# S5 of a hybrid decoder trunk with rows in the order (group, step, channel): block-diagonal products as pairs of 64x64 quadrants

## The chip, the cores and the metric

The kernel runs on one core of a Trainium2 chip. The metric is device time in microseconds (us): the median of three runs was 2262.53 us, the lowest 2256.43 and the highest 2264.71. The engines are PE (matrix products), PEld (the loading of the stationary operand into PE), DVE (vector), ACT (scalar and activation), POOL (GpSimd) and SP, whose queue issues every DMA of this kernel.

## What is computed

Two layers, 512 tokens, width 1024, float32. Each layer is a half-step FFN, a mixing sub-layer and another half-step FFN, all between RMSNorms. The mixer runs three parts on columns of one projection: A is RWKV-7 (4 heads of 64), C is a gated DeltaNet (4 heads of 128), and B, which the change touches, is S5:

```python
ug = u.reshape(bsz, t_len, S5_GROUPS, S5_GROUP_DIM)          # 16 groups of 16 channels
bu_re = jnp.einsum('btgh,gnh->btgn', ug, bbar_re)            # 64 complex states a group
bu_im = jnp.einsum('btgh,gnh->btgn', ug, bbar_im)
...
_, _, x_re, x_im = lax.associative_scan(_complex_linear_combine, elems, axis=1)
y = (jnp.einsum('btgn,ghn->btgh', x_re, c_re) - jnp.einsum('btgn,ghn->btgh', x_im, c_im)
     + d_skip.reshape(S5_GROUPS, S5_GROUP_DIM) * ug)
z = jax.nn.gelu(y.reshape(bsz, t_len, S5_WIDTH))
return z * jax.nn.sigmoid(z @ w_glu + b_glu)
```

No product of S5 crosses from one group of 16 channels to another.

## The kernel before, in words

Each layer is worked in two halves of 256 tokens, so that one half's mixer can be filled up with the other half's FFN. The string `steps` in `run` names the stages: A and B are the FFNs, P the projection, M the mixers, O the output projection, with layer and half behind the letter (M01 is layer 0, half 1). A framework's scheduler, which runs a model of the chip while the kernel is built, sets the order of the instructions on every engine. The order is fixed once built: each engine and the DMA queue of SP take theirs strictly in turn, so an instruction that has to wait holds up all behind it on its engine. A changed piece moves rows elsewhere in the program as well.

The FFN is the bulk. `up` and `down` multiply in three parts (`mm3`, lines 245 to 247): a weight tile `raw` of 256 KB comes by DMA, ACT rounds it to `whi` (line 226) and DVE computes the rest `wlo` (line 227); `ph`, `pp` and `acc` are the sums in PSUM. There are six `raw` buffers and four each of `whi` and `wlo`.

S5 takes its 256 tokens as 64 segments (`NC5`) of 4 steps (`CH5`), and its 16 groups as 8 pairs. For a pair the 128 rows of the input tile `U4` are ordered (step s, group of the pair g, channel c), 4 x 2 x 16. The state product (line 1271) multiplies 128 input rows with 128 states (2 groups x 64) for the real and the imaginary part, `lv5`; the output product (lines 1313 to 1315) goes from the two parts of the states and from `U4` to 128 output rows, with `lx5`. Since groups do not mix, half of each of these 128x128 matrices is zero. All have 64 moving columns (the segments) and are plain float32, for which the trace records two weight loads and two matmuls for each matmul of the program.

Once a layer, inside the FFN stages A00 and A10, `s5_setup` works the matrices out and stores them in DRAM (`s5w`): POOL copies each power of the matrices into zeroed tiles `Bx` and `Q` (lines 1192 and 1220), PE turns `Bx` (line 1207) and multiplies `Q` with `rep` for the tap products `pk5` (line 1238), DVE adds them to `K5` (line 1245).

In each M stage, `s5` writes its input to DRAM in eight DMAs, reads it back as `U4` in one DMA (line 1259), reads three tables (line 1264), four tiles `lv5` (line 1268) and four tiles `lx5` (line 1310), and sends its result over DRAM in four DMAs (line 1325). In the trace the digits of these names are left out: `v` is `v5` or the state product, `y` is `y5`, `U` is `U4` or `U5`.

Two helpers that S5 shares the M stage with matter for prices. `inverse2` has products of 64x64 quadrants, all in one quadrant at a time (lines 632 and 639). In `rwkv` the function `pair` (line 763) issues products of two groups of 64 rows in turn, one for each group, each into a PSUM bank of its own:

```python
ps = [self.mx([P, 2, 2, P], name) for _ in range(2)]
for j in range(2):
    for o in (1, 0):
        q = slice(64 * o, 64 * o + 64)
        m = nc.tensor.matmul(ps[o][:, j], a[q, j, c], ar[q, j, c], start=True, stop=True)
```

`inverse` sends its blocks `ATg` over DRAM (line 568, then `blk`, line 571) on the same SP queue, right behind the tables of S5.

Of the kernel before, what the change touches and what calls it, by code (L numbers as in the profile page):

```python
# [12 lines left out]
F32 = mybir.dt.float32  # L13
# [3 lines left out]
AF = mybir.ActivationFunctionType  # L17
ALU = mybir.AluOpType
AX = mybir.AxisListType

P = 128
# [6 lines left out]
DEPTH = 2  # L28
# [7 lines left out]
NC5 = HALF // CH5  # L36

R_MU, R_W0, R_A0, R_KK, R_KA, R_RK, R_V0, R_BG = 0, 8, 10, 12, 14, 16, 18, 20
R_ARE, R_AIM, R_D, R_CONV, R_LDT, R_G0, R_G2, R_G4 = 22, 30, 38, 46, 96, 0, 8, 16


class Trunk:
# [52 lines left out]
    def constants(self):  # L95
        nc, c = self.nc, self.cst
# [17 lines left out]
        self.hind = self.band(2, 64, 64, 0, "hind")  # L114
        self.bd32 = self.band(4, 32, 32, 0, "bd32")
# [14 lines left out]
    def params(self, l):  # L130
        nc, io = self.nc, self.io
        L = self.Ls[l]
        rows = self.b1([P, P], "rows")
# [17 lines left out]
        for s in range(4):  # L151
            self.late(nc.sync.dma_start(out=rows[R_D:R_D + 8, 32 * s:32 * s + 32],
                                        in_=io["s5_d"][l].rearrange("(p q) -> p q", q=32)))
# [965 lines left out]
    def s5_setup(self, l):  # L1119
        nc, io, L = self.nc, self.io, self.Ls[l]  # L1120
# [57 lines left out]
        Pw = [(self.b1([P, 8, 16], "P0r"), self.b1([P, 8, 16], "P0i"))]  # L1178
        self.cmul(Pw[0][0], Pw[0][1], b16(cr), b16(ci), Bre, Bim, [P, 8, 16])
        Cc = []  # L1180
        for cl in L["C"]:
            pc = self.mx([P, P], "pc")
            nc.tensor.transpose(pc, cl.rearrange("p t n -> p (t n)"), self.ident)
            cc = self.b1([P, 8, 16], "cc")
            nc.vector.tensor_copy(cc.rearrange("p a b -> p (a b)"), pc)
            Cc.append(cc)
        W5 = self.s5w[l]

        Bx = [self.b4([P, 8, 4, 2, 16], "Bx") for _ in range(2)]
        for t in Bx:  # L1190
            self.late(nc.gpsimd.memset(t, 0.0))
        cp = lambda o, i: nc.gpsimd.tensor_scalar(o, i, 1.0, 0.0, ALU.mult, ALU.add)
        cur = Pw[0]
        for j in range(4):
            for z in range(2):
                for g in range(2):
                    q = slice(64 * g, 64 * g + 64)
                    cp(Bx[z][q, :, 3 - j, g], cur[z][q])
            if j < 3:
                nx = (self.b1([P, 8, 16], "Pr"), self.b1([P, 8, 16], "Pi"))  # L1200
                self.cmul(nx[0], nx[1], b16(abr), b16(abi), cur[0], cur[1], [P, 8, 16])
                cur = nx
        for z in range(2):
            for hp in range(2):
                pv = self.mx([P, 4, P], "plv")
                for p in range(4):
                    nc.tensor.transpose(pv[:, p], Bx[z][:, 4 * hp + p].rearrange("n s g c -> n (s g c)"), self.ident)
                lv = self.b2([P, 4, P], "lv")
                nc.scalar.activation(lv, pv, AF.Copy)
                nc.sync.dma_start(out=W5[:, 4 * hp:4 * hp + 4, z], in_=lv)  # L1210
        Q = [[self.b4([P, 4, 5, 32], "Q") for _ in range(2)] for _ in range(2)]
        for t in Q[0] + Q[1]:
            self.late(nc.gpsimd.memset(t, 0.0))
        cur = Cc
        for j in range(5):
            for z in range(2):
                for g in range(2):
                    q = slice(64 * g, 64 * g + 64)
                    for hp in range(2):
                        nc.gpsimd.tensor_scalar(Q[z][hp][q, :, j, 16 * g:16 * g + 16], cur[z][q, 4 * hp:4 * hp + 4],  # L1220
                                                1.0 - 2 * z, 0.0, ALU.mult, ALU.add)
            if j < 4:
                nx = (self.b1([P, 8, 16], "Qcr"), self.b1([P, 8, 16], "Qci"))
                self.cmul(nx[0], nx[1], b16(abr), b16(abi), cur[0], cur[1], [P, 8, 16])
                cur = nx
        for z in range(2):
            for hp in range(2):
                nc.sync.dma_start(out=W5[:, 4 * hp:4 * hp + 4, 2 + z], in_=Q[z][hp][:, :, 1:5].rearrange("n p j c -> n p (j c)"))

        for hp in range(2):  # L1230
            pk = self.mx([P, 4, P], "pk5")
            rep = [self.b2([P, 4, 4, 32], "rep") for _ in range(2)]
            for z in range(2):
                nc.scalar.activation(rep[z], Bx[z][:, 4 * hp:4 * hp + 4, 3].rearrange("n p g c -> n p (g c)").unsqueeze(2)
                                     .to_broadcast([P, 4, 4, 32]), AF.Copy)
            for p in range(4):
                for z in range(2):
                    nc.tensor.matmul(pk[:, p], rep[z][:, p].rearrange("n s c -> n (s c)"),
                                     Q[z][hp][:, p, 0:4].rearrange("n j c -> n (j c)"), start=z == 0, stop=z == 1)
            K = self.b2([P, 4, P], "K5")  # L1240
            nc.gpsimd.tensor_tensor(K, self.ident.unsqueeze(1).to_broadcast([P, 4, P]),
                                    pr[:, R_D + 4 * hp:R_D + 4 * hp + 4].unsqueeze(2).to_broadcast([P, 4, P]), ALU.mult)
            for s in range(4):
                q = slice(32 * s, 32 * s + 32)
                nc.vector.tensor_tensor(K[q, :, 32 * s:], K[q, :, 32 * s:], pk[q, :, 0:P - 32 * s], ALU.add)
            nc.sync.dma_start(out=W5[:, 4 * hp:4 * hp + 4, 4], in_=K)


    def s5(self, l, h, I, mixT):
# [3 lines left out]
        W5 = self.s5w[l]  # L1253
# [5 lines left out]
        nc.sync.dma_start(out=U4, in_=scr.rearrange("s q p c -> (s q) p c"))  # L1259
# [48 lines left out]
        for p2 in range(4):  # L1308
            lx = self.b4([P, 2, 3, P], "lx5")
            self.after(nc.sync.dma_start(out=lx, in_=W5[:, 2 * p2:2 * p2 + 2, 2:5]), scan)  # L1310
            for p in range(2):
                q = 2 * p2 + p
# [11 lines left out]
        for t in range(4):  # L1324
            nc.sync.dma_start(out=scz[t].rearrange("p q c -> q p c"), in_=s1[32 * t:32 * t + 32])
# [193 lines left out]
```

## Time and profile before

| what | value |
|---|---|
| runs, median (lowest to highest) | 2262.53 us (2256.43 to 2264.71) |
| profiled execution, its own time | 2262.76 us |
| its span, first to last instruction | 2261.0 us |
| mean granted TensorE clock | 0.992 |
| PE, PEld, DVE, ACT, POOL busy | 97%, 90%, 75%, 53%, 7% |
| HBM read and written | 387.09 MB and 13.63 MB |

A busy share is that of recorded instructions; matmuls overlap in the pipeline, so what a matmul takes from PE is the distance to the next one's start and not its own recorded length. The M stages lie at about 325 to 500, 665 to 880, 1440 to 1660 and 1785 to 2010 us, and the two set-ups at about 115 to 185 and 1040 to 1105 us.

### The profile page before, as it was taken

How to read it: one execution, taken by the hardware profiler on the slowest of the kernel's cores; microseconds unless marked ns; L12 is line 12 of the kernel's file. 1: busy time of each engine (PE TensorE's matmuls, PEld its weight loads, DVE VectorE, ACT ScalarE, POOL GpSimd, SP SyncE). 2: the span in 40 equal slices, each digit the busy share in tenths (PEclk: the TensorE clock that was granted, in tenths of full speed). 3: DMA queues.
4: the chain of work that ended last, by engine and by line, in shares of the span. 5: the costliest groups of instructions: out<-in, count | busy, mean ns of one | idle time of the engine just before them, and what ended most of it. 6: DMA issues, size and time to landing. Idle time of an engine off the chain costs nothing.

```text
span 2261.0 us, 44455 instructions
## 1 busy us (share of the span) xinstructions
PE 2204.1 (97%) x15800; PEld 2032.1 (90%) x15800; DVE 1688.2 (75%) x3779; ACT 1191.7 (53%) x2521; POOL 163.2 (7%) x372
## 2 busy tenths in 40 slices
PE   8999999999999999999999999999999899998998
PEld 7998999897979999799989999889979799997997
DVE  6697886867876967768776678878677878677665
ACT  5555764444744444555555557544456545455554
POOL 2032000001000001201300010000020000001000
PEclk9999999999999999999999999999999999999999
DMA  7776765654765744567656677556467556456665
GB/s 207 199 209 186 186 196 151 187 145 153 202 192 154 206 136 142 175 186 220 200 177 188 189 197 204 155 172 189 130 179 207 162 172 193 123 154 187 190 187 154
DMA packets 604963, 403.67 MB, mean 179 GB/s; under 512 B 63306, under 2 KB 534340, under 8 KB 604740
## 3 DMA queue, kind: packets, MB, share of 16 engines
q1 hardware_dynamic: 604740, 400.82, 61.3%
q8 instruction: 124, 2.03, 0.4%
q14 instruction: 99, 0.81, 0.1%
HBM read 387.09 MB, written 13.63 MB: 177 GB/s over the span
## 4 chain that ended last, share of the span: by engine, by line
PE 87%; DVE 5%; DMA 4%; issue 1%; ACT 1%; POOL 0%; SPq 0%; DVEq 0%; ACTq 0%; POOLq 0%
PE ph L247 14%; PE ph L246 14%; PE ph L245 14%; PE acc L245 7%; PE acc L246 7%; PE acc L247 7%; PE pp L245 4%; PE pp L247 4%; PE pp L246 4%; PE acc L1386 2%; DVE wlo L227 1%; PE xt L309 1%; DMA blk<-scr 1%; PE py L610 1%; DMA raw<-in_w_in 1%
## 5 line engine op out<-in xcount | busy, mean ns | idle before, releaser
L226 ACT ACTIVATE whi<-raw 128x512 fp32r<-128x512 f32 (+2 forms) x1296 | 813.2, 632 | 835.4 <-PE ph L246 401.3
L227 DVE TENSOR_TENSOR wlo<-raw,whi 128x512 fp32r<-128x512 f32 (+2 forms) x1296 | 889.1, 690 | 408.5 <-ACT whi L226 397.2
L245 PE MATMUL ph<-hth,whi 128*128 128x256 f32 x2464 | 701.5, 285 | 6.1 <-DVE gu L364 3.2
L247 PE MATMUL ph<-hth,wlo 128*128 128x256 f32 x2464 | 702.4, 285 | 4.4 <-DVE wlo L227 4.1
L246 PE MATMUL ph<-htl,whi 128*128 128x256 f32 x2464 | 701.3, 285 | 3.9 <-DVE htl L318 3.8
L245 PEld LDWEIGHTS ph<-hth,whi 128*128 128x128 f32 x2464 | 466.6, 189 | 18.5 <-issue 3.9
L246 PEld LDWEIGHTS ph<-htl,whi 128*128 128x128 f32 x2464 | 466.2, 189 | 14.1 <-DVE htl L318 5.5
L247 PEld LDWEIGHTS ph<-hth,wlo 128*128 128x128 f32 x2464 | 467.2, 190 | 11.7 <-DVE wlo L227 7.5
L246 PE MATMUL acc<-wlo,gh 128*128 128x512 f32 x704 | 275.6, 397 | 0.0
L247 PE MATMUL acc<-whi,gl 128*128 128x512 f32 x704 | 271.1, 398 | 0.0
L245 PE MATMUL acc<-whi,gh 128*128 128x512 f32 x704 | 257.4, 400 | 0.6 <-ACT whi L226 0.6
L247 PEld LDWEIGHTS acc<-whi,gl 128*128 128x128 f32 x704 | 131.6, 188 | 29.4 <-issue 0.7
L246 PEld LDWEIGHTS acc<-wlo,gh 128*128 128x128 f32 x704 | 132.0, 188 | 23.4 <-issue 0.7
L245 PEld LDWEIGHTS acc<-whi,gh 128*128 128x128 f32 x704 | 130.3, 189 | 22.5 <-ACT whi L226 0.8
L245 PE MATMUL pp<-hth,whi 128*128 128x256 f32 x352 | 99.6, 284 | 2.8 <-ACT whi L226 2.5
L245 PE MATMUL ph<-hx,whi 128*128 128x256 f32 x352 | 99.3, 282 | 0.9 <-DVE gu L364 0.9
L370 ACT ACTIVATE gh<-gu 128x256 fp32r<-128x256 f32 x176 | 71.7, 407 | 52.6 <-DVE gu L364 51.7
L246 PE MATMUL pp<-htl,whi 128*128 128x256 f32 x352 | 98.9, 282 | 0.4 <-DVE htl L318 0.4
L247 PE MATMUL pp<-hth,wlo 128*128 128x256 f32 x352 | 99.0, 283 | 0.3 <-DVE wlo L227 0.2
L247 PE MATMUL ph<-hx,wlo 128*128 128x256 f32 x352 | 99.2, 282 | 0.0
L246 PE MATMUL ph<-hx,whi 128*128 128x256 f32 x352 | 98.8, 281 | 0.0
L245 PE MATMUL pp<-hx,whi 128*128 128x256 f32 x352 | 98.7, 281 | 0.0
(492 smaller groups left out, 3355.0 us busy)
## 6 DMA issues: line engine op xcount, KB each, us to landing
raw<-in_ffn_w SPq DMA_DIRECT2D x1056, 256.0 KB
raw<-in_w_in SPq DMA_DIRECT2D x176, 256.0 KB
raw<-in_w_out SPq DMA_DIRECT2D x96, 256.0 KB
raw<-in_w_in SPq DMA_DIRECT2D x32, 260.0 KB
gain<-in_norm_gain SPq DMA_DIRECT2D x28, 256.0 KB
lx<-s5w SPq DMA_DIRECT2D x16, 384.0 KB
lv<-s5w SPq DMA_DIRECT2D x16, 256.0 KB
x<-in_x SPq DMA_DIRECT2D x4, 512.0 KB
```

The source lines that it names most:

```text
L226: nc.scalar.activation(hi, q, AF.Copy)
L227: nc.vector.tensor_tensor(lo, q, hi.bitcast(F32), ALU.subtract)
L245: mm(out, lh, rh, start=start, stop=False)
L246: mm(out, lh, rl, start=False, stop=False)
L247: mm(out, ll, rh, start=False, stop=stop)
L309: self.turned = nc.tensor.transpose(pt[:, kk, i * P:(i + 1) * P], xs[i][:, k * P:(k + 1) * P], self.ident)
L370: nc.scalar.activation(gh, u, AF.Copy, scale=0.5)
L610: nc.tensor.matmul(py[:, h], ATs[z][:, h], Xs[z][:, h].rearrange("p (q e k) -> p q e k", e=2, k=32)[:, :, 0, :], start=True, stop=True)
L1386: nc.tensor.matmul(accs[i][d], mixT[:, k, s], ws[d], start=k == 0, stop=k == KT - 1)
```

## The change

The rows of a pair of groups are now ordered (group, step, channel), so that the 64 rows of one group lie together. Every matrix of S5 is then two blocks of 64x64, and only these are built, stored, loaded and multiplied: a 128x128 product becomes two 64x64 products, one in the upper left and one in the lower right quadrant of the array, written in turn. Both write the same PSUM bank, the first partitions 0 to 63 and the second 64 to 127. `U4` is read in eight DMAs of 16 rows in place of one of 128, and the result is sent out in eight in place of four. `lv5` and `lx5` come in two DMAs each in place of four, with half the bytes. In the set-up the powers go from DVE straight into `Bx` and `Q`, so the zeroing and the copies on POOL are gone; the mask `e16` takes the place of partition slices where the taps are added.

```diff
+        Bx = [self.b2([P, 8, 4, 16], "Bx") for _ in range(2)]
+        at = lambda t, j: (t[0][:, :, j], t[1][:, :, j])
+        self.cmul(*at(Bx, 3), b16(cr), b16(ci), Bre, Bim, [P, 8, 16])
+        for j in (2, 1, 0):
+            self.cmul(*at(Bx, j), b16(abr), b16(abi), *at(Bx, j + 1), [P, 8, 16])
+        Q = [self.b4([P, 8, 5, 16], "Q") for _ in range(2)]
...
-        cp = lambda o, i: nc.gpsimd.tensor_scalar(o, i, 1.0, 0.0, ALU.mult, ALU.add)
...
-                    cp(Bx[z][q, :, 3 - j, g], cur[z][q])
...
-                        nc.gpsimd.tensor_scalar(Q[z][hp][q, :, j, 16 * g:16 * g + 16], cur[z][q, 4 * hp:4 * hp + 4],
-                                                1.0 - 2 * z, 0.0, ALU.mult, ALU.add)
...
+            self.cmul(*at(Q, j + 1), b16(abr), b16(abn), *at(Q, j), [P, 8, 16])
...
-                for z in range(2):
-                    nc.tensor.matmul(pk[:, p], rep[z][:, p].rearrange("n s c -> n (s c)"),
-                                     Q[z][hp][:, p, 0:4].rearrange("n j c -> n (j c)"), start=z == 0, stop=z == 1)
+        halves = (slice(0, 64), slice(64, P))
+        for p in range(8):
             for z in range(2):
+                for q in halves:
+                    nc.tensor.matmul(pk[q, p], rep[z][q, p].rearrange("n s c -> n (s c)"),
+                                     Q[z][q, p, 0:4].rearrange("n j c -> n (j c)"), start=z == 0, stop=z == 1)
...
-                nc.vector.tensor_tensor(K[q, :, 32 * s:], K[q, :, 32 * s:], pk[q, :, 0:P - 32 * s], ALU.add)
+            nc.vector.scalar_tensor_tensor(K[:, :, 16 * s:], pk[:, :, 0:64 - 16 * s], self.e16[:, s:s + 1], K[:, :, 16 * s:],
+                                           ALU.mult, ALU.add)
...
-        nc.sync.dma_start(out=U4, in_=scr.rearrange("s q p c -> (s q) p c"))
+        for g in range(2):
+            for s in range(4):
+                nc.sync.dma_start(out=U4[64 * g + 16 * s:64 * g + 16 * s + 16], in_=scr[s, 16 * g:16 * g + 16])
...
-        for p2 in range(4):
-            lv = self.mw.tile([P, 2, 2, P], F32, tag="lv5", name=self.n("lv5"), bufs=4)
-            self.after(nc.sync.dma_start(out=lv, in_=W5[:, 2 * p2:2 * p2 + 2, 0:2]), I["usi"])
-            for p in range(2):
+        for hp in range(2):
+            lv = self.mw.tile([P, 4, 2, 64], F32, tag="lv5", name=self.n("lv5"), bufs=4)
+            self.after(nc.sync.dma_start(out=lv, in_=WV[:, 4 * hp:4 * hp + 4]), I["usi"])
+            for p in range(4):
                 for z in range(2):
-                    nc.tensor.matmul(pv[z][:, 2 * p2 + p], lv[:, p, z], U4[:, 2 * p2 + p], start=True, stop=True)
+                    for q in halves:
+                        nc.tensor.matmul(pv[z][q, 4 * hp + p], lv[q, p, z], U4[q, 4 * hp + p], start=True, stop=True)
...
-                nc.tensor.matmul(py[:, q], lx[:, p, 2], U4[:, q], start=True, stop=False)
-                nc.tensor.matmul(py[:, q], lx[:, p, 0], X[0][:, q, 0:NC5], start=False, stop=False)
-                nc.tensor.matmul(py[:, q], lx[:, p, 1], X[1][:, q, 0:NC5], start=False, stop=True)
+                for k, m in ((2, U4[:, i]), (0, X[0][:, i, 0:NC5]), (1, X[1][:, i, 0:NC5])):
+                    for q in halves:
+                        nc.tensor.matmul(py[q, i], lx[q, p, k], m[q], start=k == 2, stop=k == 1)
...
-        for t in range(4):
-            nc.sync.dma_start(out=scz[t].rearrange("p q c -> q p c"), in_=s1[32 * t:32 * t + 32])
+        for g in range(2):
+            for t in range(4):
+                nc.sync.dma_start(out=scz[t, :, 16 * g:16 * g + 16].rearrange("p q c -> q p c"),
+                                  in_=s1[64 * g + 16 * t:64 * g + 16 * t + 16])
```

The order on PE around the state products of M00, before. A row is line, operation, output and inputs, and size of the output; `v` has two tiles, one for the real and one for the imaginary part.

```order
L246 MATMUL ph_6179<-htl_3072,whi_6188 128x256
L1271 MATMUL v_1085_4928<-U_1081_4920,lv_1087_4930 128x64 x2
L1271 MATMUL v_1085_4928<-U_1081_4920,lv_1088_4936 128x64 x2
L1271 MATMUL v_1085_4928<-U_1081_4920,lv_1089_4942 128x64 x2
L1271 MATMUL v_1085_4928<-U_1081_4920,lv_1090_4948 128x64 x2
L247 MATMUL ph_6179<-hth_3071,wlo_6189 128x256
```

The same place in the change: first the place where the first product of the state stands, then the one where the others begin.

```order
L250 MATMUL ph_6151<-hth_2957,whi_6190 128x256
L251 MATMUL ph_6151<-htl_2958,whi_6190 128x256
L1257 MATMUL v_1060_4864<-U_1056_4849,lv_1062_4866 64x64
L252 MATMUL ph_6151<-hth_2957,wlo_6191 128x256
L250 MATMUL ph_6151<-hth_2961,whi_6190 128x256
```

```order
L251 MATMUL ph_6151<-htl_2984,whi_6196 128x256
L1257 MATMUL v_1060_4864<-U_1056_4849,lv_1062_4866 64x64 x6
L1257 MATMUL v_1061_4865<-U_1056_4849,lv_1062_4866 64x64 x6
L1257 MATMUL v_1060_4864<-U_1056_4849,lv_1062_4866 64x64
L1257 MATMUL v_1061_4865<-U_1056_4849,lv_1062_4866 64x64 x2
L1257 MATMUL v_1060_4864<-U_1056_4849,lv_1063_4884 64x64 x2
```

One product of the upper quadrant now stands alone, 12 FFN matmuls ahead of the other 31, which follow one another with the two quadrants in turn. So it is in all four M stages (7 to 12 matmuls ahead). The output products stand as two pairs alone and then 22 pairs in one piece, where before two single ones were followed by pieces of 10 and 12, or of 10, 6 and 6.

The order on SP around the input of S5 in M00, before; a row's last part is the size of the destination.

```order
L221 DMA raw_6292<-in_ffn_w 128x4x128
L1259 DMA U_1081_4920<-s5u_4911 128x512
L1264 DMA T_1082_4922<-s5t_127 128x512
L1264 DMA U_1083_4923<-s5t_128 128x512
L1264 DMA M_1084_4924<-s5t_129 128x512
L221 DMA raw_6322<-in_ffn_w 128x4x128
L221 DMA raw_6328<-in_ffn_w 128x4x128
L221 DMA raw_6367<-in_ffn_w 128x512
L568 DMA scr_4834<-ATg_4786 32x8x32 x4
L571 DMA blk_4843<-scr_4834 64x1024
```

And in the change:

```order
L226 DMA raw_6264<-in_ffn_w 128x4x128
L1244 DMA U_1056_4849<-s5u_4840 16x512 x8
L1249 DMA T_1057_4858<-s5t_136 128x512
L1249 DMA U_1058_4859<-s5t_137 128x512
L1249 DMA M_1059_4860<-s5t_138 128x512
L573 DMA scr_4763<-ATg_4715 32x8x32 x4
L226 DMA raw_6294<-in_ffn_w 128x4x128
L226 DMA raw_6300<-in_ffn_w 128x4x128
L576 DMA blk_4772<-scr_4763 64x1024
```

One issue for `U4` has become eight, and no weight tile stands between the tables and `ATg`, where three did.

## Rows read from the trace of the kernel before

**Rows 1.** The page, part 1: busy time, share and instructions of each engine.
```profile
PE 2204.1 (97%) x15800; PEld 2032.1 (90%) x15800; DVE 1688.2 (75%) x3779; ACT 1191.7 (53%) x2521; POOL 163.2 (7%) x372
```

**Rows 2.** The page, part 4: shares of the chain that ended last.
```profile
PE 87%; DVE 5%; DMA 4%; issue 1%; ACT 1%; POOL 0%; SPq 0%; DVEq 0%; ACTq 0%; POOLq 0%
```

**Rows 3.** Groups by line: busy us, mean ns, then idle us before them and releaser.
```profile
L1271 PE MATMUL v<-U,lv 128*128 128x64 f32 x128 | 15.1, 271 | 0.0
...
L1313 PE MATMUL y<-U,lx 128*128 128x64 f32 x64 | 12.1, 270 | 1.6 <-DMA lx<-s5w 1.5
L1238 PE MATMUL pk<-Q,rep 128*128 128x128 f32 x64 | 11.3, 351 | 4.3 <-POOL Q L1220 4.3
```

**Rows 4.** PE in order of time, M00, state products: start us, length us, instruction.
```profile
390.21 0.28 PE L246 MATMUL ph<-htl,whi 128*128 128x256 f32 x1
390.33 1.89 PE L1271 MATMUL v<-U,lv 128*128 128x64 f32 x16
392.03 0.36 PE L247 MATMUL ph<-hth,wlo 128*128 128x256 f32 x1
```

**Rows 5.** PE in order of time, M00, output products: a piece of 20 records.
```profile
417.70 0.33 PE L1315 MATMUL y<-X5i,lx 128*128 128x64 f32 x2
...
419.85 0.48 PE L247 MATMUL acc<-whi,gl 128*128 128x512 f32 x1
```

**Rows 6.** PE in order of time, products of one 64x64 quadrant, M00 and M01.
```profile
491.44 0.28 PE L246 MATMUL ph<-htl,whi 128*128 128x256 f32 x1
491.64 1.14 PE L632 MATMUL py<-xb,AT 64*64 64x64 f32 x16
492.71 0.39 PE L247 MATMUL ph<-hth,wlo 128*128 128x256 f32 x1
...
825.48 2.08 PE L639 MATMUL pz<-W,Y 64*64 64x64 f32 x32
827.48 0.38 PE L247 MATMUL ph<-hth,wlo 128*128 128x256 f32 x1
```

**Rows 7.** PE in order of time: two row groups in turn, then one row group alone.
```profile
333.83 1.13 PE L763 MATMUL pk<-ar,ka 64*128 64x256 f32 x8
334.90 0.39 PE L245 MATMUL ph<-hth,whi 128*128 128x256 f32 x1
...
1430.98 1.12 PE L729 MATMUL pv<-vr,wv 32*128 32x256 f32 x4
1432.04 0.55 PE L715 MATMUL pn<-ident,rkk 128*128 128x128 f32 x3
```

**Rows 8.** PE in order of time, set-up of layer 0: transposes, then tap products.
```profile
160.95 1.09 PE L1207 MATMUL plv<-ident,Bx 128*128 128x128 f32 x8
161.79 0.37 PE L247 MATMUL ph<-hth,wlo 128*128 128x256 f32 x1
...
173.39 5.24 PE L1238 MATMUL pk<-Q,rep 128*128 128x128 f32 x30 [2.15 <-POOL Q L1220]
178.39 0.36 PE L247 MATMUL ph<-hth,wlo 128*128 128x256 f32 x1
```

**Rows 9.** DVE in order of time, set-up of layer 0: the last powers of `Q`.
```profile
169.52 0.28 DVE L1070 TENSOR_TENSOR Qci<-Qci,cm 128x128 f32<-128x128 f32 x1
```

**Rows 10.** SP's queue and PE in order of time, M00 and M10.
```profile
383.91 0.48 SPq L1259 DMA_DIRECT2D U<-s5u  x1
384.45 0.42 SPq L1264 DMA_DIRECT2D T<-s5t  x1
384.92 0.42 SPq L1264 DMA_DIRECT2D U<-s5t  x1
...
1496.00 0.49 SPq L1259 DMA_DIRECT2D U<-s5u  x1
...
1501.09 1.89 PE L1271 MATMUL v<-U,lv 128*128 128x64 f32 x16
```

**Rows 11.** The chain that ended last, in order of time: a piece of M00.
```profile
391.95 2.75 DMA scr<-ATg
```

More of the change, by code (lines that the diff above doesn't have):

```diff
@@ L151, in params @@
         for s in range(4):
-            self.late(nc.sync.dma_start(out=rows[R_D:R_D + 8, 32 * s:32 * s + 32],
-                                        in_=io["s5_d"][l].rearrange("(p q) -> p q", q=32)))
+            self.late(nc.sync.dma_start(out=rows[R_D:R_D + 8].rearrange("p (g s c) -> p g s c", g=2, s=4)[:, :, s],
+                                        in_=io["s5_d"][l].rearrange("(p g c) -> p g c", g=2, c=16)))
         put(R_CONV, io["gdn_conv_w"][l].rearrange("i (t c) -> (i t) c", c=P), 48)
@@ L1182, in s5_setup @@
+        Q = [self.b4([P, 8, 5, 16], "Q") for _ in range(2)]
+        for z, cl in enumerate(L["C"]):
             pc = self.mx([P, P], "pc")
             nc.tensor.transpose(pc, cl.rearrange("p t n -> p (t n)"), self.ident)
[L1184 to L1191, printed above, removed]
@@ new lines, in s5_setup @@
+        pk = self.mx([P, 8, 64], "pk5")
+        rep = [self.b2([P, 8, 4, 16], "rep") for _ in range(2)]
+        for z in range(2):
+            nc.scalar.activation(rep[z], Bx[z][:, :, 3].unsqueeze(2).to_broadcast([P, 8, 4, 16]), AF.Copy)
+        halves = (slice(0, 64), slice(64, P))
+        for p in range(8):
+            for z in range(2):
+                for q in halves:
+                    nc.tensor.matmul(pk[q, p], rep[z][q, p].rearrange("n s c -> n (s c)"),
+                                     Q[z][q, p, 0:4].rearrange("n j c -> n (j c)"), start=z == 0, stop=z == 1)
@@ L1258, in s5 @@
         U4 = self.b2([P, 8, NC5], "U4")
-        nc.sync.dma_start(out=U4, in_=scr.rearrange("s q p c -> (s q) p c"))
+        for g in range(2):
+            for s in range(4):
+                nc.sync.dma_start(out=U4[64 * g + 16 * s:64 * g + 16 * s + 16], in_=scr[s, 16 * g:16 * g + 16])
         T = self.b2([P, 8, NC5], "T5")
@@ L1307, in s5 @@
         py = self.mx([P, 8, NC5], "y5")
[L1308 to L1312, printed above, removed]
-                nc.tensor.matmul(py[:, q], lx[:, p, 2], U4[:, q], start=True, stop=False)
-                nc.tensor.matmul(py[:, q], lx[:, p, 0], X[0][:, q, 0:NC5], start=False, stop=False)
-                nc.tensor.matmul(py[:, q], lx[:, p, 1], X[1][:, q, 0:NC5], start=False, stop=True)
+        for hp in range(2):
+            lx = self.b4([P, 4, 3, 64], "lx5")
+            self.after(nc.sync.dma_start(out=lx, in_=WX[:, 4 * hp:4 * hp + 4]), scan)
+            for p in range(4):
+                i = 4 * hp + p
+                for k, m in ((2, U4[:, i]), (0, X[0][:, i, 0:NC5]), (1, X[1][:, i, 0:NC5])):
+                    for q in halves:
+                        nc.tensor.matmul(py[q, i], lx[q, p, k], m[q], start=k == 2, stop=k == 1)
         s1, s2 = self.b2([P, 8, NC5], "ge1"), self.b2([P, 8, NC5], "ge2")
@@ L1432, in run @@
         self.vf = [self.dr.tile([P, 2, HALF], F32, name=f"vf{h}", tag=f"vf{h}") for h in range(2)]
-        self.s5w = [self.dr.tile([P, 8, 5, P], F32, name=f"s5w{l}", tag=f"s5w{l}") for l in range(DEPTH)]
+        self.s5w = [self.dr.tile([P, 8, 3, 64], F32, name=f"s5w{l}", tag=f"s5w{l}") for l in range(DEPTH)]
+        self.s5v = [self.dr.tile([P, 8, 2, 64], F32, name=f"s5v{l}", tag=f"s5v{l}") for l in range(DEPTH)]
         s5t = [[self.dr.tile([P, 512], F32, name=f"s5t{l}{i}", tag=f"s5t{l}{i}") for i in range(3)] for l in range(DEPTH)]
```

71 lines of the change are left out of this document (24 added, 47 removed).

## The prediction, made before the changed kernel ran

> **What bounds the kernel.** I read the page's busy shares first, then the chain of work that ended last, then the groups by line, and then PE's and SP's rows in order of time at the places that the change touches. PE is busy 2204.1 us of a span of 2261.0 us, so it is idle for 56.9 us in the whole program [rows 1], and 87% of the chain that ended last is PE [rows 2]. In the M stages PE fills the waits of the mixers with FFN products, so what a product of S5 takes from PE delays the FFN behind it. So I price the change by PE's time, as the distance between starts, and look for new waits that break PE's fixed order. The sum is made against the profiled execution's own 2262.76 us, which is 0.23 us above the median.
>
> **State and output products.** The program has 64 state products, which the trace records as 128 [rows 3], 32 an M stage. Sixteen of them take 390.33 to 392.03, 1.70 us, or 0.106 us each [rows 4]. The output products are three lines of 64 records, 48 an M stage; 20 of them take 417.70 to 419.85, 0.1075 us each [rows 5]. Before: 32 x 0.106 + 48 x 0.1075 = 8.56 us an M stage.
>
> Now there are twice as many records, of 64x64. Products in one quadrant are in the trace: 16 take 1.07 us to the next start and 32 take 2.00 us, so each more costs (2.00 - 1.07) / 16 = 0.058 us [rows 6]. What is left, 1.07 - 16 x 0.058 = 0.14 us, is the price of a piece, and its first product starts 0.20 us behind the FFN's last where a full one starts 0.12 us behind [rows 4, 6]: together 0.22 us a piece.
>
> Whether the two quadrants of a pair run together decides the sum. The kernel has products that alternate between two groups of 64 rows: eight records with 256 moving columns take 1.07 us to the next start. Four such records in one row group take 1.06 us [rows 7]. So the second group costs nothing there. I take the same for the quadrants: a slot of two records of one product and two of its partner takes 2 x 0.058 = 0.116 us. By the order an M stage has five pieces: one product alone, 31 in 16 slots, two single pairs, and 22 pairs, 41 slots in all. Now: 41 x 0.116 + 5 x 0.22 = 5.86 us, a gain of 2.70 us an M stage and **10.8 us** in four. If they take turns, the stage has 160 x 0.058 + 1.1 = 10.4 us, 1.8 us more than before; these are the two ends, and I take the first, since [rows 7] is the only row with alternating groups.
>
> One difference remains: those products have a PSUM bank for each row group, these have one bank for both, on different partitions. The Trainium skill, page TensorEngine Tiling (Array Packing), section Restrictions and Gotchas, says that different row tiles cannot access the same PSUM bank simultaneously. No row of this trace shows two row groups on one bank, so the trace neither bears it out nor speaks against it; by that rule the stage would be 1.8 us longer and not 2.7 us shorter, the first rival below.
>
> **Tap products.** Thirty records take 173.39 to 178.39, 5.00 us [rows 8]; with two that stand apart 5.2 us a layer. Now 16 slots and a piece: 16 x 0.116 + 0.22 = 2.1 us. Gain 3.1 us a layer, **6.2 us**. PE also waits 2.15 us for POOL's copies into `Q` [rows 8], 4.3 us in both layers [rows 3]. DVE has the last power ready at 169.80 [rows 9], and PE comes to its wait at 173.39 - 2.15 = 171.24, so without the copies the data is there. But the new order puts the products six rows earlier, some 0.7 us by FFN starts 0.12 us apart [rows 4], and DVE writes them in strided tiles. Bounds 0 and 4.3 us, I take **3.2 us**. POOL's memsets and copies otherwise hid behind DVE and PE; at nothing.
>
> **Transposes.** Eight take 0.84 us [rows 8], 32 in all 3.4 us. Their weights have half the columns, their moving side is as long as before: between nothing and half, 0 and 1.7 us; I take **0.7 us**, nearer to nothing, since the moving side is unchanged.
>
> **Loads of lx.** PE waits 1.5 us for them in all [rows 3]. Half the bytes and two issues in one place: 0 to 1.5 us, I take **1.0 us**. DVE's tap sums are one chain in place of two, hidden behind PE; if that cover is gone, they are a gain.
>
> **What the change adds: SP.** `U4` takes eight issues. Issues of the tables follow 0.47 us apart [rows 10], so its last piece goes out 3.3 us behind the first, and the tables, `ATg` and the weight tiles behind it come 3.3 us later. PE starts the state products 6.4 us behind the issue of `U4` in M00 and 5.1 us in M10 [rows 4, 10], without a wait. A small transfer lands 2.75 us after its issue [rows 11], so the last piece lands 3.3 + 2.75 = 6.05 us after the first issue: no wait in M00, 1.0 us in M10. I count one of each for the other half of the tokens: 2 us. What stands behind it on PE is FFN work, all of it in order. For the later weights and the inverse the bounds are 0 and 3.3 us a stage, 13 us; six weight buffers stand ahead of PE, so I take 0.5 us a stage, 2 us. Together **4 us lost**. Four more issues on the way out (1.9 us a stage) delay only the end of S5; at nothing, since the inverse is still running then; 1.9 us a stage if it is not.
>
> **Sum.** -10.8 - 6.2 - 3.2 - 0.7 - 1.0 + 4.0 = -17.9 us: 2244.9 us, or about **2245 us** for the median. All bounds on the good side give -24.5 us (2238), all on the bad side with the pairs still together -17 + 15 = -2 us (2261), and some us more with the outgoing DMAs.
>
> **Rivals.**
> 1. *The quadrants take turns.* Then +1.82 us an M stage, 7.3 us; the tap products 64 x 0.058 + 0.22 = 3.9 us, still 1.3 us less a layer, 2.6 us; with the other terms (-3.2 - 0.7 - 1.0 + 4.0) it gives +3.8 us, 2266.5 us: slower than before. It would be worse if each change of quadrant cost the 0.14 us of a piece's end: some 80 changes a stage and 32 a set-up, 54 us, 2320 us. For it: the shared bank. Against it: [rows 7]. There are 4 x 41 + 2 x 16 = 196 slots, so the change turns slower from a slot of 0.116 + 17.9 / 196 = 0.21 us on. Chance 0.13.
> 2. *SP comes late.* If a piece of `U4` takes over 3.1 us from issue to landing, PE waits in all four stages, and the inverse behind it, 3.3 us late, is waited for too: 6.6 us a stage, 26 us in place of 4, which gives 2267 us. For it: the eight issues, and `ATg` close behind. Against it: PE had no wait there before, and FFN work fills the place. Chance 0.10.
> 3. *The gain is given back elsewhere.* The scheduler has moved rows in all M stages, and PE's 56.9 us of idle time can grow by as much as the products shrink. Half of it: about 2254 us. For it: every order on PE holds up all behind it. Against it: the scheduler fills with the same FFN products. Chance 0.15.
>
> **Chances.** The forecast has 0.62. A measurement can tell about 0.5%, 11.3 us: faster is below 2251, slower above 2274. The forecast lies beyond 2251 in nine of ten of its cases, and a fifth of rival 3 does: faster 0.59. Rivals 1 and 2 at their own times are within 0.5%; their bad ends give slower 0.08; the rest, 0.33, is no change. The range 2237 to 2266 holds the forecast with its bounds, rival 3, and the near ends of 1 and 2.
>
> **What would show it.** The state products of a stage with starts of pairs some 10 ns apart and 0.116 us from slot to slot, some 2.1 us for the 31; the set-up's tap products in about 2 us with no wait for POOL; S5's 128*128 products gone from PE in favour of 64*64 ones, and PE's busy time down by 15 to 20 us. It is wrong if quadrants start 0.058 us apart, if PE waits for `U` by over 1 us a stage, or if FFN rows wait longer for `wlo` and `whi`.

## The result and the profile after

Six runs of the changed kernel have a median of 2238.57 us (2235.08 to 2239.64); six of the kernel before, on the same chip, 2261.05 us (2256.43 to 2264.71). The ratio is 0.990, 95% interval 0.9887 to 0.9914: 22.5 us less, where 17.5 were forecast. By the half per cent that the prediction took as what a measurement can tell, the change is **faster**, by 1.0%, and the time lies in its range. The profiled execution took 2235.08 us, the fastest of its six, with a span of 2233.4 us. Against the profiled one of before it is 27.7 us less; 22.5 us is the figure to explain, and the mean granted clock (0.996 against 0.992) is part of the difference between the two: the clock has the levels 2.4 and 1.2 GHz, so as an estimate the means stand for 18 us at the lower one, against 36 us before (2 x 0.004 x 2233.4 and 2 x 0.008 x 2261.0).

Page of the changed kernel, part 1 and part 4's shares of the chain that ended last:

```profile
PE 2180.9 (98%) x16184; PEld 2001.4 (90%) x16184; DVE 1673.9 (75%) x3773; ACT 1191.4 (53%) x2517; POOL 106.2 (5%) x250
...
PE 87%; DVE 5%; DMA 4%; issue 2%; ACT 1%; SPq 1%; POOL 0%; DVEq 0%; ACTq 0%; POOLq 0%
```

Against [rows 1, 2]: PE is busy 23.2 us less (15 to 20 were named as a sign) although it has 384 records more, POOL 57 us less, and the chain is PE's by the same 87%. So PE's occupancy is still what is to be added up.

PE of the changed kernel in order of time in M00 (start us, length us, instruction; one output row is one slot of two records in each quadrant):

```profile
385.57 0.33 PE L1257 MATMUL v<-U,lv 64*64 64x64 f32 x2
...
387.25 0.28 PE L251 MATMUL ph<-htl,whi 128*128 128x256 f32 x1
387.46 2.08 PE L1257 MATMUL v<-U,lv 64*64 64x64 f32 x62
389.46 0.39 PE L252 MATMUL ph<-hth,wlo 128*128 128x256 f32 x1
...
413.07 0.33 PE L1301 MATMUL y<-X5i,lx 64*64 64x64 f32 x4
413.24 0.28 PE L1301 MATMUL y<-U,lx 64*64 64x64 f32 x4
...
415.57 0.28 PE L1301 MATMUL y<-X5i,lx 64*64 64x64 f32 x4
```

Sixty-two records of state products take 2.00 us to the FFN's next start, and 20 slots of output products take 413.24 to 415.57, 0.1165 us each. A slot holds one 64x64 product of each quadrant, and one such product alone took as long in the kernel before (two records of 0.058 us [rows 6]); a whole 128x128 product took 0.21 us, two records of 0.106 [rows 4]. In the single records of M00 the second quadrant starts 6 to 7 ns behind the first. Two quadrants on one PSUM bank, on different partitions, run together, in all four M stages. The rule of the Trainium skill that the prediction weighed (TensorEngine Tiling (Array Packing), Restrictions and Gotchas: different row tiles cannot access one PSUM bank simultaneously) did not show in the time: the measurement decides.

Set-up of layer 0, PE of the changed kernel in order of time:

```profile
169.93 2.08 PE L1220 MATMUL pk<-Q,rep 64*64 64x64 f32 x64
171.94 0.24 PE L130 MATMUL grt<-ident,grows 24*128 24x24 f32 x1
```

All 32 tap products of the layer (64 records) take 2.01 us, without a wait, where [rows 8] had 30 of the 32 records of before in 5.00 us behind a wait of 2.15.

But these 5.00 us were not all products. Windows of the kernel before (stretch, its length, busy us and instructions of PE, PEld, DVE, ACT and POOL, then granted clock, DMA share, GB/s), the wait and the tap products in layer 0, and those of layer 1:

```profile
170.00:173.40 3.40, 1.25 (x12) 1.04 (x10) 3.16 (x4) 1.95 (x5) 3.17 (x5) 1.00 0.56 165
173.40:178.40 5.00, 5.00 (x31) 5.00 (x31) 1.94 (x4) 0.00 (x0) 3.60 (x18) 0.66 0.35 102
...
1095.30:1100.30 5.00, 4.97 (x30) 4.97 (x31) 1.93 (x4) 0.00 (x0) 3.64 (x18) 0.66 0.35 100
```

Right behind the wait for POOL the granted clock is 0.66 in the mean, a mixture of the two levels 2.4 and 1.2 GHz. I had priced the records of that stretch as if they ran at full clock. In the changed kernel the same place has 1.00; its tap products, 169.93 to 171.94, lie across two windows:

```profile
165.00:170.80 5.80, 5.80 (x68) 5.44 (x67) 4.96 (x16) 3.91 (x7) 0.21 (x2) 1.00 0.59 160
170.80:173.00 2.20, 2.20 (x50) 2.10 (x47) 1.39 (x4) 0.00 (x0) 0.10 (x1) 1.00 1.00 231
```

What got worse, by the waits of PE in the changed kernel (us in total, times, longest), and the two longest of M01 in order of time:

```profile
PE ph L252 <- DVE wlo L232: 5.9, 6, 1.9
PE y L1301 <- DMA lx<-s5w: 2.9, 3, 1.6
```

```profile
717.25 0.38 PE L252 MATMUL ph<-hth,wlo 128*128 128x256 f32 x1 [1.89 <-DVE wlo L232]
723.83 0.33 PE L1301 MATMUL y<-U,lx 64*64 64x64 f32 x4 [1.61 <-DMA lx<-s5w]
```

The kernel before waits 1.5 us for lx [rows 3] and 4.1 us for that wlo:

```profile
PE ph L247 <- DVE wlo L227: 4.1, 8, 1.6
```

The two waits of M01, 3.5 us, take more than the 3.0 us that its products gain; by the FFN products on either side, the stage took 1.4 us longer than before. Over all lines that show such a wait, those for wlo grew from 5.2 to 7.0 us and those for whi fell from 7.9 to 4.4: of the prediction's last sign of being wrong one half came, and the two together fell. PE waits for `U4` nowhere, though SP issues it as priced (SP's queue, M00):

```profile
378.71 3.69 SPq L1244 DMA_DIRECT2D U<-s5u  x8
382.50 1.24 SPq L1249 DMA_DIRECT2D T<-s5t  x1
```

In M10 the first piece goes out at 1475.66 us, and PE shows, again without a wait:

```profile
1480.80 0.33 PE L1257 MATMUL v<-U,lv 64*64 64x64 f32 x2
...
1483.25 0.97 PE L1257 MATMUL v<-U,lv 64*64 64x64 f32 x25
```

### The profile page after: what moved, and what is told of

Same layout as the page of the kernel before. It is cut to its first block, busy times and chain, and to the rows that moved or that the text cites. A ratio compares the mean times of both kernels' runs of the same rounds, so it can differ in the third digit from the quotient of the medians.

```text
span 2233.4 us, 45076 instructions
## 1 busy us (share of the span) xinstructions
PE 2180.9 (98%) x16184; PEld 2001.4 (90%) x16184; DVE 1673.9 (75%) x3773; ACT 1191.4 (53%) x2517; POOL 106.2 (5%) x250
## 4 chain that ended last, share of the span: by engine, by line
PE 87%; DVE 5%; DMA 4%; issue 2%; ACT 1%; SPq 1%; POOL 0%; DVEq 0%; ACTq 0%; POOLq 0%
PE ph L252 14%; PE ph L250 14%; PE ph L251 14%; PE acc L251 7%; PE acc L250 7%; PE acc L252 7%; PE pp L252 4%; PE pp L250 4%; PE pp L251 4%; PE acc L1374 2%; DVE wlo L232 2%; DMA blk<-scr 1%; PE xt L314 1%; DMA raw<-in_ffn_w 1%; PE py L615 1%
## 5 line engine op out<-in xcount | busy, mean ns | idle before, releaser
L250 PE MATMUL ph<-hx,whi 128*128 128x256 f32 x352 | 98.9, 281 | 0.9 <-DVE gu L369 0.9
L250 PE MATMUL pp<-hx,whi 128*128 128x256 f32 x352 | 98.5, 280 | 0.0
L251 PE MATMUL pp<-hx,whi 128*128 128x256 f32 x352 | 98.5, 280 | 0.0
```

Of the source, the lines that this page charges most:

```text
L250: mm(out, lh, rh, start=start, stop=False)
L251: mm(out, lh, rl, start=False, stop=False)
```

## Experiments

Times are medians; "before" ran on the same chip in each group. Occupancy is the sum over all four stages (or two set-ups) of the distance from a record to PE's next start, from the trace. In the changed kernel it is 9.04 us for the state products, 12.94 us for the output products and 4.02 us for the tap products.

**First group** (before: 2260.57 us). *The quadrants apart*: all products of the upper quadrant, then all of the lower.

```diff
-            for p in range(4):
-                for z in range(2):
-                    for q in halves:
+        for q in halves:
+            for i in range(8):
+                for z in range(2):
```
(the output products likewise)

> The changed kernel with the same 64x64 products in another order: in each M stage all products of the upper quadrant first, then all of the lower one, for the state and for the output products. Theory (the gain in the M stages is that the two quadrants of a pair run together): each record now takes 0.058 us by itself, so the 160 records of a stage take 160 x 0.058 + 5 pieces x 0.2 = 10.3 us against 5.5 us in the changed kernel: 4.8 us a stage, 19 us in all, about 2258 us. Rival (the gain comes from the set-up, from the halved bytes or from the new order of other work): the products of a stage may take what they will, the time stays within 3 us of 2239. Second rival (PE's queue finds partners across eight or more instructions by itself): no change in the starts, two records some 7 ns apart.

Measured: 2249.86 us (2246.74 to 2255.61; ratio 0.9951, 0.9934 to 0.9967), 11.3 us over the changed kernel. PE in order of time in M00:

```profile
416.72 0.33 PE L1309 MATMUL y<-X5i,lx 64*64 64x64 f32 x2
416.88 0.28 PE L1309 MATMUL y<-U,lx 64*64 64x64 f32 x2
417.00 0.28 PE L1309 MATMUL y<-X5r,lx 64*64 64x64 f32 x2
...
422.05 0.38 PE L252 MATMUL ph<-hth,wlo 128*128 128x256 f32 x1
```

A product alone takes the 0.1165 us that a pair took. Occupancy is 15.32 + 23.53 us, 16.9 us more than with the quadrants in turn and 4.8 us more than in the kernel before (13.62 + 20.44). So the gain in the M stages hangs on the pairs. The four runs lie 9 us apart, and why the median rose by less than the occupancy is open.

*Full matrices in the M stages*: the new order of rows and the new set-up, but 128x128 matrices with zero halves, loaded and multiplied whole.

```diff
-                    for q in halves:
-                        nc.tensor.matmul(pv[z][q, 4 * hp + p], lv[q, p, z], U4[q, 4 * hp + p], start=True, stop=True)
+                    nc.tensor.matmul(pv[z][:, 2 * p2 + p], lv[:, p, z], U4[:, 2 * p2 + p], start=True, stop=True)
...
+                nc.sync.dma_start(out=WV[r, :, z, o], in_=nil[r])
```

> The changed kernel with its set-up and its row order, but the M stages again load full 128x128 matrices with zero halves (in four DMAs each, twice the bytes) and multiply them as one product; the zero halves are written to DRAM once a layer. Theory: the products of a stage take the 8.5 us of the kernel before in place of 5.5, 3.0 us a stage, 12 us in all, about 2251 us; the set-up keeps its gain. Rival (the set-up and its consequences are the whole gain): within 3 us of 2239. Other rival (the set-up gives nothing of its own): about 2260, as before.

Measured: 2267.48 us (2266.05 to 2272.46; ratio 1.0035, 1.002 to 1.005), 29 us over the changed kernel. Occupancy rose by 12.5 us, where 12 were foreseen; most of the rest came from how the zero halves were written. Windows in set-up 0, columns as above:

```profile
140.00:145.00 5.00, 2.03 (x17) 1.82 (x16) 2.60 (x9) 0.65 (x2) 0.10 (x1) 1.00 0.77 194
145.00:150.00 5.00, 2.96 (x12) 2.56 (x12) 3.62 (x10) 2.92 (x5) 0.00 (x0) 0.64 0.96 307
150.00:155.00 5.00, 5.00 (x25) 4.61 (x24) 2.12 (x7) 1.78 (x4) 0.21 (x2) 0.67 0.74 248
```

The DMAs that fill the zero halves stood on SP among the weight loads; PE lost 5.0 us in two waits for whi, and right behind them the clock fell. By FFN products on either side, this place cost 8.25 us, and the one in set-up 1 6.55 us.

*POOL copies back in the set-up*: tap matrices and powers go through 56 copies a layer on POOL again.

```diff
-        for j in range(4):
-            self.cmul(*at(Q, j + 1), b16(abr), b16(abn), *at(Q, j), [P, 8, 16])
...
+                    for hp in range(2):
+                        hold(Q[z][64 * g:64 * g + 64, 4 * hp:4 * hp + 4, j], cur[z][64 * g:64 * g + 64, 4 * hp:4 * hp + 4])
```

> The changed kernel with the copies on POOL put back in the set-up: DVE makes each power in a tile of its own and POOL copies it into Bx and Q in the pieces of before; the quadrant products stay. Theory: PE waits for POOL again ahead of the tap products, 2.15 us a layer, and if the clock is granted at half behind such a wait as before, some 1.7 us more a layer: 4 to 8 us slower than the changed kernel, 2243 to 2246 us, with the wait back in the profile and the tap products still 2 us for 64 records at full clock. Rival (the set-up gained only by the smaller products): no change, within 2 us of 2239.

Measured: 2243.44 us (2238.24 to 2243.63; ratio 0.9921, 0.9905 to 0.9937), 4.9 us more, inside the range of the theory, but not by the way that it names. Waits of PE for POOL:

```profile
PE plv L1224 <- POOL Bx L1188: 2.3, 2, 1.2
...
PE pk L1239 <- POOL Q L1188: 0.4, 2, 0.2
```

Ahead of the tap products PE waits 0.2 us a layer and not 2.15, and the granted clock stays at 1.00 in both set-ups. The wait has moved ahead to the transposes, and the tap products, now in four pieces, take 5.31 us in place of 4.02: 2.3 + 0.4 + 1.3 = 4.0 us.

*U4 read in one DMA*:

```diff
-        for g in range(2):
-            for s in range(4):
-                nc.sync.dma_start(out=U4[64 * g + 16 * s:64 * g + 16 * s + 16], in_=scr[s, 16 * g:16 * g + 16])
+        nc.sync.dma_start(out=U4, in_=scr.rearrange("g s c p t -> (g s c) p t"))
```
(and `scr` written in 16 pieces for 8)

> The changed kernel with the input of S5 written to DRAM in the order (group, step, channel), in 16 pieces early in the stage in place of 8, and read back in one DMA in place of eight. Theory (PE never waited for the input, and FFN work covers what is late on SP): no change, within 2 us of 2239, with the tables, ATg and blk some 3 us earlier on SP. Rival (the eight issues hold up all that is behind them on SP, and the stages M00 and M01 lose by it): 3 to 8 us faster, 2231 to 2236 us.

Measured: 2234.64 us (2232.98 to 2238.39; ratio 0.989, 0.9874 to 0.9906). The wait for lx fell from 2.9 to 1.2 us. The median is 3.9 us under that of the changed kernel and in the rival's range, and M01, by the FFN products on either side, took 2.3 us less than in the kernel before. But the interval overlaps that of the changed kernel: a gain is likely, not shown.

**Second group** (before: 2260.04 us). *One U4 read and lx let go earlier*: `first = V(Zr, pv[0], T, ALU.mult)`, and the loads of lx follow `first` in place of `scan`.

> The changed kernel with two edits: U4 read back in one DMA (written in 16 pieces), as in the run before that measured 2234.6 us, and the loads of the output matrices (lx) let go when the first rotation of the states has run, instead of waiting for the scan. In the changed kernel TensorE waited 2.9 us for lx in all, 1.6 of it in one stage (the second head block of layer 0), which gained nothing; with the single U4 read alone 1.2 us were left. Theory (the lx waits lie on the path): these 1.2 us go too, 2232.5 to 2235 us, at most 0.3 us of lx waits left. Rival (the earlier loads push the weight loads behind them on SP, and TensorE waits for those): 2235 to 2238 us, with waits for raw, whi or wlo grown by 1 us or more.

Measured: 2232.48 us (2228.49 to 2236.65; ratio 0.9876, 0.9858 to 0.9894), the lowest median of all. But the reason given did not hold: lx is still waited for, 1.4 us in all. PE in order of time in M01:

```profile
716.32 0.33 PE L1301 MATMUL y<-U,lx 64*64 64x64 f32 x4 [1.14 <-DMA lx<-s5w]
732.88 0.33 PE L1301 MATMUL y<-X5r,lx 64*64 64x64 f32 x4
```

The scheduler has moved the first output piece, which needs only U4 and lx, forward along with the load.

*The kernel before with its copies on ACT*: one edit to the kernel before, to price POOL's copies without the quadrants.

```diff
-                        nc.gpsimd.tensor_scalar(Q[z][hp][q, :, j, 16 * g:16 * g + 16], cur[z][q, 4 * hp:4 * hp + 4],
-                                                1.0 - 2 * z, 0.0, ALU.mult, ALU.add)
+                        nc.scalar.activation(Q[z][hp][q, :, j, 16 * g:16 * g + 16], cur[z][q, 4 * hp:4 * hp + 4],
+                                             AF.Copy, scale=1.0 - 2 * z)
```

> The kernel before, with one edit: the forty copies a layer that put C times powers of A into Q move from GpSimd to ScalarE; the tap products stay 128x128 with their zero halves. Theory (5.0 us of tap products a layer held a wait of 2.15 us for GpSimd and, right behind it, a stretch at half clock): the wait goes and the 30 products run at about 0.116 us each instead of 0.171, so 2.15 + 1.7 us a layer come back, 7.7 us in two layers: 2251 to 2255 us against 2260.8 for the kernel before, at a granted clock of 1.00 in the stretch of the tap products. Rival 1 (the wait is only moved: VectorE or ScalarE is late next, or the clock falls there anyway): 2258 to 2261 us. Rival 2 (ScalarE falls behind with its weight copies): slower than 2262 us.

Measured: 2255.80 us (eleven runs, 2254.39 to 2259.69; ratio 0.9985, 0.9975 to 0.9996): 4.2 us less, where 7.7 were expected, and just outside the theory's range. PE in order of time in layer 0, and the window of the tap products:

```profile
172.94 3.96 PE L1238 MATMUL pk<-Q,rep 128*128 128x128 f32 x32
...
184.37 0.38 PE L247 MATMUL ph<-hth,wlo 128*128 128x256 f32 x1 [0.89 <-DVE wlo L227]
```

```profile
173.40:178.40 5.00, 5.00 (x38) 4.69 (x39) 2.06 (x4) 4.84 (x15) 0.60 (x6) 1.00 0.80 227
```

The wait and the low clock are gone, as the theory has it: the full 128x128 products now run at 0.114 us each (7.28 us of occupancy for 64, for 10.28) at a clock of 1.00. That saves 1.5 us a layer beside the 2.15 us wait, 7.3 us in two layers. Part is given back: ACT is busy 4.84 of 5.00 us, and PE then waits 0.29 and 0.89 us for wlo; between the FFN products around it, layer 0 gained 2.4 us and layer 1 2.6 us.

*Full matrices with their fills aside*: as above, with the zero fills on POOL's queue, early.

```diff
-                nc.sync.dma_start(out=WV[r, :, z, o], in_=nil[r])
+                self.late(nc.gpsimd.dma_start(out=WV[r, :, z, o], in_=nil[r]))
```

> As the run with full 128x128 matrices in the head-block stages (2267.5 us), but with the ten DMAs a layer that fill the zero halves issued from GpSimd's queue early on, not from SP's queue among the weight loads. The run before was 29 us over the changed kernel, where the products' own occupancy explains 12.5; in its two set-ups some 8 and 6.5 us were lost at one place, where TensorE waited 3.0 + 2.0 us for a weight load and then ran at half clock. Theory (zero halves cost the products' occupancy and not much else; the rest was the fills in SP's queue): 2250 to 2255 us, no wait of over 1 us for whi in the set-ups. Rival (the doubled bytes of the matrices in the head-block stages are what costs): 2260 to 2268 us, with the excess in the four head-block stages.

Measured: 2249.16 us (2245.44 to 2253.68; ratio 0.9951, 0.9936 to 0.9966), 10.6 us over the changed kernel and just under the 2250 to 2255 expected. PE in order of time in M00:

```profile
385.94 3.68 PE L1268 MATMUL v<-U,lv 128*128 128x64 f32 x32
```

Occupancy is 13.95 + 20.70 us, 12.7 us more than with quadrants. So the zero halves are worth their occupancy and little else; the doubled bytes of lv and lx cost nothing that shows.

*Runs of two and three* in a quadrant before the other's turn, for state and output products, in this order by force.

```diff
+        for i in range(8):
+            for q in halves:
+                for z in range(2):
...
```

> The changed kernel with the quadrants in runs: state products in the order 0 1 1 0 0 1 1 0, output products 0 0 0 1 1 1 0 0 0 1 1 1, instead of 0 1 0 1. Theory (instructions start in program order, a quadrant takes one product at a time at 0.116 us, and only neighbours of different quadrants run together): the state products keep their pairs, 16 slots a stage, no change; six output products take 4 slots instead of 3, so 32 slots instead of 24, 0.93 us more a stage, 3.7 us in four stages: 2241 to 2244 us, y products 16.7 us instead of 12.9, v 9.0. Rival 1 (TensorE looks ahead past a waiting product): no change, 2238.6 within 2, y 12.9. Rival 2 (each change of quadrant must find the other empty): both lists fall back to one at a time, as with the quadrants apart, about 2250 us, v 15.3 and y 23.5.

Measured: 2237.27 us (2234.39 to 2238.86; ratio 0.9897, 0.988 to 0.9913), occupancy 9.07 and 13.70 us: rival 1 but for 0.8 us, and the theory fell. PE in order of time in M00; the order in the program is X5i in the upper quadrant, U, X5r, X5i in the lower, U, X5r, X5i in the upper:

```profile
413.90 0.27 PE L1309 MATMUL y<-X5i,lx 64*64 64x64 f32 x1
413.91 0.27 PE L1309 MATMUL y<-U,lx 64*64 64x64 f32 x1
414.01 0.22 PE L1309 MATMUL y<-X5i,lx 64*64 64x64 f32 x1
414.02 0.22 PE L1309 MATMUL y<-U,lx 64*64 64x64 f32 x1
414.07 0.22 PE L1309 MATMUL y<-X5r,lx 64*64 64x64 f32 x1
414.08 0.27 PE L1309 MATMUL y<-U,lx 64*64 64x64 f32 x1
414.13 0.22 PE L1309 MATMUL y<-X5r,lx 64*64 64x64 f32 x1
414.19 0.22 PE L1309 MATMUL y<-U,lx 64*64 64x64 f32 x1
414.19 0.22 PE L1309 MATMUL y<-X5i,lx 64*64 64x64 f32 x1
```

The upper quadrant's second U starts at 414.08, 0.11 us ahead of the lower quadrant's X5i that stands before it in the program. So over this distance a product that waits for its quadrant does not hold the next one for the other quadrant. PE waited 5.0 us for lx in this run, 2.1 us more than in the changed kernel, and the median is no higher: what such a wait costs is not its length.

**Third group** (before: 2261.48 us). *The changed kernel again*, unedited, as the base of this group:

> The changed kernel once more, unedited, beside the two runs that mean to better it. Expected at 2238.6 us as before, between 2236 and 2241.

Measured: 2237.11 us (2235.11 to 2243.28; ratio 0.9893, 0.9875 to 0.991), the same within the intervals.

*The U4 product last* of the three of an output block, so that no early piece needs only `U4` and lx.

```diff
-                for k, m in ((2, U4[:, i]), (0, X[0][:, i, 0:NC5]), (1, X[1][:, i, 0:NC5])):
+                for k, m in ((0, X[0][:, i, 0:NC5]), (1, X[1][:, i, 0:NC5]), (2, U4[:, i])):
```
(and the flags `start` and `stop` to match)

> The changed kernel with one edit: of the three products of an output block, the one with U4 comes last instead of first, so that nothing can need lx before the states are there. In the changed kernel each stage has one early piece of one output pair of U4, and it is this piece that waits for lx (2.9 us in all). In the run with the earlier loads the early piece came earlier by as much (at 716.8 us instead of 724.8 in the second stage) and waited again (1.4 us in all). Theory (the early piece makes the wait): the lx waits go, and four pieces with them at about 0.22 us each, so 2.9 + 0.9 = 3.8 us: 2233.5 to 2236 us, no wait for lx over 0.3 us. Rival (the place on TensorE is only taken by waits for weights): 2237 to 2240 us.

The rows that the expectation means by 724.8 and 716.8 us stand in the traces at 723.83 and 716.32. Measured: 2234.83 us (2233.0 to 2241.1; ratio 0.9884, 0.9867 to 0.9901). No wait for lx is left, and the output products take 12.36 us for 12.94; the time is in the theory's range and 2.3 us under the changed kernel beside it, but the intervals overlap.

*One U4 read and the U4 product last*, both edits:

> U4 read back in one DMA (2234.6 us alone) and the U4 product last. Theory (the two gains add up as far as the lx waits go: 1.2 us were left with the single U4 read, and four pieces at 0.22): 2231.5 to 2234 us. Rival (the rest of the gain is eaten by waits for weight loads and VectorE): 2234 to 2237 us.

Measured: 2236.23 us (2233.63 to 2236.6; ratio 0.9883, 0.987 to 0.9897): rival. The lx waits are gone here too, while wlo (4.9 us) and whi (3.8 us for one FFN line) remain. The two gains do not add up.

*Runs of four and twelve*, in the manner of the runs of two and three, in a single run:

> How far TensorE looks ahead: the changed kernel with runs of four state products and of twelve output products in one quadrant before the other's turn. Runs of two and three kept all pairs (62 records of the state products inside 1.86 us), runs of sixteen and twenty-four kept none (15.3 and 23.5 us in four stages). Theory (the other quadrant's products start while at most some four products wait ahead of them): the state products stay at 9 to 10 us in four stages; the output products overlap by three to four slots at each of three changes of quadrant, so 4 x (5.57 - 3 x 0.4) = 17 to 18 us with their pieces some 20 us. Rival 1 (it looks ahead by twelve or more): y stays near 13 to 14 us. Rival 2 (by two or three only): v 11 to 13 us and y 21 us or more.

Measured: 2251.1 us in one run; occupancy 11.02 us for the state and 21.79 us for the output products: the numbers of rival 2, a shorter look ahead than I had thought. PE in order of time at the first change of quadrant in M00:

```profile
418.25 0.28 PE L1309 MATMUL y<-U,lx 64*64 64x64 f32 x2
418.36 0.22 PE L1309 MATMUL y<-X5r,lx 64*64 64x64 f32 x1
418.37 0.27 PE L1309 MATMUL y<-U,lx 64*64 64x64 f32 x1
418.42 0.22 PE L1309 MATMUL y<-X5r,lx 64*64 64x64 f32 x1
418.47 0.22 PE L1309 MATMUL y<-U,lx 64*64 64x64 f32 x1
418.48 0.22 PE L1309 MATMUL y<-X5i,lx 64*64 64x64 f32 x1
418.53 0.22 PE L1309 MATMUL y<-X5r,lx 64*64 64x64 f32 x1
418.54 0.22 PE L1309 MATMUL y<-X5i,lx 64*64 64x64 f32 x1
418.59 0.22 PE L1309 MATMUL y<-X5r,lx 64*64 64x64 f32 x1
418.65 0.28 PE L1309 MATMUL y<-X5i,lx 64*64 64x64 f32 x2
```

Rows with x2 are one quadrant alone; from 418.36 to 418.59 the last records of the one run lie beside the first three of the other. So each change saves three records, 3 x 0.058 = 0.175 us. That accounts for all the orders: in runs of three products (six records) three overlap at either end, and everything is paired; 46 products in runs of twelve take 46 x 0.1165 - 3 x 0.175 = 4.83 us, measured 4.82 from first to last; in runs of sixteen and twenty-four next to nothing is saved.

## Why the prediction was right, and where it was not

| step | predicted, us | in the trace, us |
|---|---|---|
| state and output products | -10.8 | -12.1 (34.06 to 21.98) |
| tap products | -6.2 | -6.3 (10.28 to 4.02) |
| POOL wait | -3.2 | -4.3 (4.3 to 0) |
| transposes | -0.7 | -0.1 (3.27 to 3.16) |
| loads of lx | -1.0 | +1.4 (1.5 to 2.9) |
| SP and U4 | +4.0 | no wait for U4; the rest not separated, 0 to 4 |
| sum | -17.9 | -21.4 without SP and U4; medians -22.5 |

- **State and output products: right.** Pairs take one slot of 0.1165 us, as two row groups took the time of one in [rows 7], though the group alone there has 32 rows and not 64. A stage takes 5.5 us in place of the 5.86 forecast. With the quadrants apart the gain in occupancy is gone and more; with full matrices 10.6 us of time is lost again, by 12.7 us of occupancy.
- **Tap products: the right sum, half of it for another reason.** Of the 3.1 us a layer, 1.5 are the clock, which fell right behind the wait for POOL; that the sum came out is luck, since these came back only with the wait gone. The kernel before with its copies on ACT shows it: the same full products took 3.6 us a layer. The zero halves alone are worth 1.6 us a layer. The step that failed is "Thirty records take 173.39 to 178.39, 5.00 us", taken as their price: 0.167 us a record, half as much again as the 0.106 us of [rows 4], should have sent me to the granted clock.
- **POOL wait: the upper bound.** I took 3.2 of 4.3 us because the products came six rows earlier; all of the wait went.
- **Transposes: the lower bound.** With half the weight columns and the same 128 moving ones they cost nearly what they did, 3.16 us for 3.27.
- **lx: the wrong sign.** I counted fewer bytes and issues, and not that the early piece of output products is placed by the scheduler close behind the load. With the earlier load the piece moved along; with the U4 product last the wait was gone. The bounds had left out a loss, without a reason to.
- **SP and U4: the wait that was priced did not come, and what came in its place is not settled.** For M10 I forecast 1.0 us of waiting, since PE would start 5.1 us behind the first issue and the last piece would land at 6.05. PE does start 5.1 us behind it (1475.66 to 1480.80), but this is the lone product of the upper quadrant, which reads only the 64 rows whose four pieces go out first; the lower rows are first read at 1483.25, 7.6 us behind, and in the other stages 7.6 to 8.8. The order in the section on the change showed this, and my sum left it out. What the eight issues delay is lx and weights, in M01 above all. In sum, the run with one read lies 3.9 us lower, close to the 4.0 forecast though by another way, and 1.7 us of waits for lx, which the row above counts too, went with it. With the U4 product last, one read gained nothing (2234.83 and 2236.23 us). So the term lies somewhere from 0 to 4 us, as far as these medians tell.

The chances put 0.62 on this mechanism, and of the rivals none came. For rival 1, the quadrants taking turns, the price can be read from the run with them apart: 16.9 us of occupancy over the pairs, and 4.8 us over the kernel before, where the rival had 7.3.

The lowest median is that of the changed kernel with one U4 read and earlier lx loads, 2232.48 us, 1.24% under the kernel before (interval 1.06% to 1.42%) against 1.0% for the change alone. The difference between the two is about 5 us, and their intervals overlap a little (0.9858 to 0.9894, and 0.9887 to 0.9914), so that it betters the changed kernel is likely, not shown.

## What to carry to other kernels

Block-diagonal products are worth splitting into quadrants if the two halves alternate closely: in this kernel a pair costs what one of its 64x64 products costs alone, 0.1165 us, and runs of up to three in one quadrant lose next to nothing (22.77 us of occupancy for 21.98), while runs of sixteen and twenty-four cost more (38.85) than the full products of before (34.06). Before pricing a block of products by its rows, look at the granted clock of its window: a wait just ahead can have made them look dearer than they are. And give an early piece of work no operand that arrives late; a scheduler that fills gaps will place it right behind the load.

## What the runs showed that was not expected

- Products for different quadrants start out of program order over a short distance: at a change of quadrant three records, 0.175 us, overlap. So what the section on the kernel before says, that an instruction that waits holds up all behind it on its engine, does not hold on PE across quadrants.
- The granted clock fell to a mean of 0.64 to 0.67 right behind waits of 2.15 us (POOL, kernel before, both layers) and of 3.0 + 2.0 us (whi, full matrices), and was 1.00 at the same places in the kernels without the wait. The loss behind the wait for POOL was 1.5 us a layer on top of 2.15. Not every wait of this length does it: with the runs of two and three PE waited 2.8 us for lx in M01, and the 5 us behind it show 1.00.
- Transposes with 64 weight columns cost nearly what those with 128 cost (32 take 3.16 us against 3.27).
